# Gate/up blocks with four quads each, two pairs of the up half split by ScalarE and an adding DMA

## The chip, the cores and the metric

One core of a Trainium2 chip runs the whole layer. The metric is the device time of one execution in microseconds (us); lower is better. Durations in the text come from one profiled execution of the kernel before.

## What is computed

The input x has 256 tokens of 2048 channels. Three stages follow each other, each with a norm ahead of it and behind it and a residual sum: a feed-forward stage, a mixer (a recurrent branch and a pooling branch) and a second feed-forward stage. The change touches the gate and up products of the two feed-forward stages:

```
f = (silu(u @ w_gate) * (u @ w_up)) @ w_down     # u: 256 x 2048, normed
                                                 # w_gate, w_up: 2048 x 5632, w_down: 5632 x 2048
h = h + 0.5 * rmsnorm(f) * g
```

## The kernel before

**Products in three parts.** All weights are float32. TensorE multiplies them in its float32r form, which keeps fewer bits, so each operand is split into a high part H (the value rounded to float32r) and a low part L = value - H. A product of two tiles is three matmuls into one PSUM bank (`mm3`, L313 to L315): H by H, L by H, H by L. The weight is the moving operand: 128 rows by 512 columns, against 128 tokens.

**How a weight tile comes in.** `fetch` (L356) handles a *pair*: two neighbouring groups of 128 weight rows by 512 columns. SP loads the 512 KB (`get_w`, L275), ScalarE writes H as a rounding copy (`cast`, L367), VectorE subtracts for L (`low`, L370). The load goes into one of four w32 buffers or a spare *unit* (a 128 x 1024 tile from a pool of 33); H and L go into a ring of five buffers, or, with `hold`, into two units of their own.

**Gate/up blocks.** The 5632 columns are 11 blocks of 512. Block 0 is a plain product. Blocks 1 to 10 go through `seven` (L482 on), which computes one block of gate (f) and of up (l) together for both halves of the 256 tokens, four output tiles of 128 x 512. The string in `GATE_UP` gives the order within a block: `f` is a pair of gate (12 matmuls), `l` a pair of up, `q` a *quad*. A quad takes two groups of 128 rows of both gate and up and computes what a pair of each would, but with seven products in place of eight: 21 matmuls against 24. For that it needs sums and differences of the weights. SP loads four pieces of 256 KB (L545), VectorE makes t13 (L550, 1024 per partition), and the two halves of t24 (L555 and L559, 512 each), ScalarE casts four operands (L567) and VectorE subtracts for four low parts (L572, three of 1024 and one of 512). With n quads a block has 8 - n pairs of f and of l. Blocks 2, 4, 6, 8 and 10 have three quads, blocks 3, 5, 7 and 9 four.

**The rest of a block.** `merge` copies the first finished product (L614, ScalarE, once per block) and adds others to it (L619, six additions per block, VectorE); `total` (L666) closes the up half. Then come silu (L1020), the product of both halves (L1027), a transposition in 32 x 32 squares (L848, VectorE), sixteen moves of 32 KB between partitions by GpSimd's DMAs (`move`, L865), and the split of the result into H and L (L878 ScalarE, L882 VectorE), which stays in units as the operand of the down product.

**What sets the order.** A planner (`Plan`, L87 on) lists every instruction of these stages as a node with an engine, an assumed duration, its inputs, the buffers it takes and frees, and a due time counted back from TensorE's order, which is fixed. `solve` (L134) places the nodes one by one: on each engine the one that can start first, by due time where several can. The instructions of PE, ScalarE, VectorE and SP are then emitted in that order (`run`, L261). GpSimd is not among the engines of that hand-made schedule; its order is left to the framework. For a DMA the planner assumes a start `LEAVE` after the issue, a rate of `RATE` MB per us on one shared line, and `LAND` until the data can be used.

Of the kernel before, what the change touches and what calls it, by code (L numbers as in the profile page):

```python
# [10 lines left out]
F32 = mybir.dt.float32  # L11
# [45 lines left out]

ROWS = [("ln_mix_pre", 16), ("ln_ffn2_pre", 16), ("mu", 26), ("w0", 8), ("a0", 8),
        ("k_k", 8), ("k_a", 8)]
# [27 lines left out]
class Plan:  # L87
# [46 lines left out]
    def solve(s):  # L134
        succ = {n: [] for n in s.nodes}
        for n in s.nodes:
            for d in n.deps:
                succ[d].append(n)
        for n in reversed(s.nodes):
            for m in succ[n]:  # L140
                if n.eng == "PE":
                    break
                v = m.due - n.dur - (n.lat + (EARLY if m.eng == "PE" else 0.0)
                                     if m.eng != n.eng else 0.0)
# [70 lines left out]
class Block:  # L215
# [45 lines left out]
    def run(s):  # L261

        E = mybir.EngineType
        with s.tc.manual_schedule(engines={E.PE, E.Activation, E.DVE, E.SP}):
            for n in s.plan.solve():
                n.fn()
            s.stats()
        s.plan, s.ready = Plan(), {}
# [84 lines left out]
            for h in range(2):  # L353
                evac(h, pss[h])

    def fetch(s, w, k, c0, keep, hold=False):  # L356

        p, x = s.plan, {}
        src = Tok("w32", "unit")
        dst = [Tok("unit"), Tok("unit")] if hold else [Tok("ring")]  # L360

        def load():
            x["w"] = s.get_w(w, k, 2, c0, 512, own=src.of == "unit")

        def cast():
            x["v"], x["H"], x["L"] = s.halves_of(x["w"], hold)
            s.nc.scalar.copy(x["H"], x["v"])  # L367

        def low():
            s.nc.vector.tensor_tensor(out=x["L"], in0=x["v"], in1=x["H"].bitcast(F32),  # L370
                                      op=ALU.subtract)
# [110 lines left out]
    def seven(s, wf, cf, wl, cl, at, dep, KT, need, sm, order, ev_f, ev_l, used, trail=0):  # L482
# [32 lines left out]
        def keep(tiles):  # L515
            ws.update((k, (wH, wL)) for k, wH, wL in tiles)

        def pair(k, w, c0, b):
            low, dst = s.fetch(w, k, c0, keep)

            def do():
                for i in range(2):
# [6 lines left out]
        def quad(q):  # L529
# [40 lines left out]
            def low(n_, m):  # L570
# [1 line left out]
                V.tensor_tensor(out=L, in0=src, in1=H.bitcast(F32), op=ALU.subtract)  # L572
                x[n_] = [(H[:, i], L[:, i]) for i in range(m)]
            ld = [p.op("SP", 0.4, lambda m=m: get(m), take=([ka], [kb], (), ())[m], size=0.26,
                       chain="SP") for m in range(4)]

            def half(n_, m, deps, rel):
                ring = Tok("ring")
# [56 lines left out]
        for c in order:  # L635
            if c == "q":
                last["q"] = quad(nq)
                nq += 1
                if nq == n:
                    merge(last["q"])  # L640
                    if "f" in m:
                        close_f()
                continue
            w_ = (wf, cf) if c == "f" else (wl, cl)
            last[c] = pair(next(ks[c]), *w_, c)
# [208 lines left out]
    def carry_steps(s, T1, T, x32=None):  # L854
# [1 line left out]
        nc = s.nc  # L856
        x, own = [x32], []

        def move():
            if x32 is None:  # L860
                x[0] = s.unit((P, 4, 2, 4, 32), F32, "x32")
            src = s.blocks(T1[0])
            for i in range(4):
                for q in range(4):
                    nc.gpsimd.dma_start(out=x[0][q * 32:q * 32 + 32, i],  # L865
                                        in_=src[i * 32:i * 32 + 32, q])
# [26 lines left out]
    def carry(s, T1, T, turned, k1):  # L893
# [1061 lines left out]
```

## Time and profile before

| | us |
|---|---|
| median of 3 runs | 2025.65 (2025.48 to 2026.15) |
| the profiled execution | 2025.32 |
| its span, first to last instruction | 2023.6 |

The profile gives for each engine its busy time and, for groups of equal instructions, the count and mean duration; the chain that ended last; the windows, which are busy times of each engine in a stretch of the span; and the timeline, which has single instructions with their start and length. Lines such as L370 are lines of the kernel before. Matmuls overlap on TensorE and VectorE's instructions overlap a little, so the distance of two starts is the price of an instruction in a full engine, and the duration is more than that.

### The profile page before, as it was taken

What the parts mean: (1) busy time and instruction counts of PE and PEld (TensorE: products, weight loads), DVE (VectorE), ACT (ScalarE), POOL (GpSimd) and SP (SyncE); (2) the same over time, 40 slices, a digit from 0 to 9 for tenths busy, and PEclk for the clock granted to TensorE, in tenths of its full rate; (3) what the DMA queues carried; (4) which work ended last, traced back from release to release, by engine and by line L of the source; (5) the groups of instructions that cost most, each with busy time, mean ns of one, the idle gap of its engine ahead of it and who ended that gap; (6) DMA issues with size and microseconds to landing.
All of it is one profiled execution on the core that took longest, in us unless ns stands there. A gap on an engine that the chain in (4) does not pass through costs nothing.

```text
span 2023.6 us, 28609 instructions
## 1 busy us (share of the span) xinstructions
PE 2008.3 (99%) x9987; PEld 1660.2 (82%) x9987; DVE 1774.4 (88%) x2344; ACT 1180.8 (58%) x1575; POOL 325.2 (16%) x673
## 2 busy tenths in 40 slices
PE   9999999999999999999999999999999999999997
PEld 7888888888888888888788788888888888888886
DVE  6999999999989857799689577779999999999896
ACT  7565665655655566685576434565566556566553
POOL 0111211121000123403220111011112111210000
PEclk9999999999999999999999999999999999999999
DMA  7757475577567677757456558756574755775674
GB/s 267 254 179 265 148 253 188 186 221 245 185 204 268 225 204 214 204 175 216 147 169 187 160 169 278 245 196 232 187 266 151 246 190 183 223 243 189 203 261 145
DMA packets 227098, 423.55 MB, mean 209 GB/s; under 512 B 24320, under 2 KB 27786, under 8 KB 226954
## 3 DMA queue, kind: packets, MB, share of 16 engines
q1 hardware_dynamic: 204393, 384.70, 58.5%
q0 software_dynamic: 22272, 36.51, 5.5%
q8 instruction: 78, 1.28, 0.3%
q10 hardware_dynamic: 288, 0.52, 0.1%
q14 instruction: 67, 0.54, 0.1%
HBM read 396.69 MB, written 8.39 MB: 200 GB/s over the span
## 4 chain that ended last, share of the span: by engine, by line
PE 98%; issue 1%; DVE 1%; ACT 0%; DMA 0%; DVEq 0%; POOLq 0%; POOL 0%; SPq 0%; ACTq 0%
PE mm L313 27%; PE mm L315 27%; PE mm L314 27%; PE ms L313 4%; PE ms L315 4%; PE ms L314 4%; PE tr L822 0%; PE pA L1673 0%; PE mc L790 0%; PE pU L1769 0%; DMA w<-in_ffn_gate_dram 0%; PE pSa L1781 0%; PE pY L1804 0%; DVE xL L840 0%; PE pT L1840 0%
## 5 line engine op out<-in xcount | busy, mean ns | idle before, releaser
L313 PE MATMUL mm<-wH,xH 128*128 128x512 f32 (+1 forms) x2184 | 851.5, 391 | 0.4 <-ACT xH L831 0.4
L315 PE MATMUL mm<-wH,xL 128*128 128x512 f32 (+1 forms) x2184 | 847.8, 388 | 1.6 <-DVE xL L840 1.6
L314 PE MATMUL mm<-wL,xH 128*128 128x512 f32 (+1 forms) x2184 | 847.5, 388 | 0.0
L367 ACT CAST wH<-w 128x1024 fp32r<-128x1024 f32 x333 | 346.8, 1053 | 239.7 <-PE mm L315 209.2
L315 PEld LDWEIGHTS mm<-wH,xL 128*128 128x128 f32 x2184 | 409.9, 188 | 87.5 <-DVE xL L840 3.2
L313 PEld LDWEIGHTS mm<-wH,xH 128*128 128x128 f32 x2184 | 410.0, 188 | 85.5 <-ACT xH L831 1.0
L314 PEld LDWEIGHTS mm<-wL,xH 128*128 128x128 f32 x2184 | 410.1, 188 | 82.3
L370 DVE TENSOR_TENSOR wL<-w,wH 128x1024 fp32r<-128x1024 f32 x333 | 396.9, 1217 | 39.5 <-ACT wH L367 36.5
L567 ACT CAST wH<-t 128x1024 fp32r<-128x1024 f32 x188 | 198.2, 1054 | 222.8 <-PE mm L315 156.5
L290 DVE TENSOR_TENSOR wL<-w,wH 128x1024 fp32r<-128x1024 f32 (+2 forms) x202 | 239.0, 1192 | 96.5 <-ACT wH L289 93.3
L289 ACT CAST wH<-w 128x1024 fp32r<-128x1024 f32 (+2 forms) x202 | 207.7, 1034 | 164.5 <-PE mm L315 142.9
L865 POOL DMA_DIRECT2D x<-T x352 | 172.5, 498 | 748.4 <-DVE T L848 394.9
L572 DVE TENSOR_TENSOR wL<-t,wH 128x1024 fp32r<-128x1024 f32 x188 | 225.5, 1217 | 14.1 <-ACT wH L567 13.9
L567 ACT CAST wH<-w 128x1024 fp32r<-128x1024 f32 (+1 forms) x188 | 153.6, 835 | 48.4 <-PE mm L315 40.3
L572 DVE TENSOR_TENSOR wL<-w,wH 128x1024 fp32r<-128x1024 f32 (+1 forms) x188 | 175.6, 950 | 2.4 <-ACT wH L567 2.4
L550 DVE TENSOR_TENSOR t<-w,w 128x1024 f32<-128x1024 f32 x94 | 114.4, 1217 | 0.7 <-DMA w<-in_ffn_down_dram 0.7
L313 PE MATMUL ms<-wH,sH 128*128 128x512 f32 x252 | 98.0, 389 | 0.0
L314 PE MATMUL ms<-wL,sH 128*128 128x512 f32 x252 | 98.0, 389 | 0.0
L315 PE MATMUL ms<-wH,sL 128*128 128x512 f32 x252 | 98.0, 389 | 0.0
L559 DVE TENSOR_TENSOR t<-w,t 128x512 f32<-128x512 f32 x94 | 64.8, 689 | 2.1
L555 DVE TENSOR_TENSOR t<-w,t 128x512 f32<-128x512 f32 x94 | 64.3, 684 | 0.8
L619 DVE TENSOR_TENSOR u<-ms,u 128x512 f32<-128x512 f32 x92 | 61.3, 685 | 1.6
(311 smaller groups left out, 2017.6 us busy)
## 6 DMA issues: line engine op xcount, KB each, us to landing
w<-in_w_in_dram SPq DMA_DIRECT2D x128, 512.0 KB
w<-in_ffn_down_dram SPq DMA_DIRECT2D x116, 512.0 KB
w<-in_ffn_up_dram SPq DMA_DIRECT2D x114, 512.0 KB
w<-in_ffn_gate_dram SPq DMA_DIRECT2D x112, 512.0 KB
w<-in_ffn_gate_dram SPq DMA_DIRECT2D x128, 256.0 KB
w<-in_ffn_up_dram SPq DMA_DIRECT2D x124, 256.0 KB
w<-in_ffn_down_dram SPq DMA_DIRECT2D x120, 256.0 KB
w<-in_w_out_dram SPq DMA_DIRECT2D x28, 512.0 KB
```

The source lines that it names most:

```text
L289: s.nc.scalar.copy(vH, v)
L290: s.nc.vector.tensor_tensor(out=vL, in0=v, in1=vH.bitcast(F32), op=ALU.subtract)
L313: nc.tensor.matmul(ps, aH, bH, start=start, stop=False)
L314: nc.tensor.matmul(ps, aH, bL, start=False, stop=False)
L315: nc.tensor.matmul(ps, aL, bH, start=False, stop=stop)
L367: s.nc.scalar.copy(x["H"], x["v"])
L370: s.nc.vector.tensor_tensor(out=x["L"], in0=x["v"], in1=x["H"].bitcast(F32), op=ALU.subtract)
L550: V.tensor_tensor(out=v["t13"], in0=v["a"], in1=v["b"][:, :1].to_broadcast([P, 2, 512]), op=ALU.subtract)
L559: V.tensor_tensor(out=v["t24"][:, 1], in0=v["b"][:, 1], in1=v["t24"][:, 0], op=ALU.subtract)
L567: nc.scalar.copy(H, src)
L572: V.tensor_tensor(out=L, in0=src, in1=H.bitcast(F32), op=ALU.subtract)
L865: nc.gpsimd.dma_start(out=x[0][q * 32:q * 32 + 32, i], in_=src[i * 32:i * 32 + 32, q])
```

## The change

Blocks 2 to 9 all have the order `ffqfqfqlqLLl`: four quads, four pairs of gate, and four pairs of up, of which two, written `L`, get their low part in another way. ScalarE writes H as before and then -1 times the weight, rounded, into the tile of L (that is -H); a DMA that GpSimd issues then adds the same weights, read once more from DRAM, to that tile, so it holds value - H. VectorE has no part in it. These two pairs have H and L in units of their own (`hold`), not in the ring, and their casts are not in the chain that keeps the other casts in order.

Beside it: GpSimd joins the engines whose order the planner writes out; the sixteen moves of a block become four steps of four; a load may be placed no earlier than `FETCH` = 22 us ahead of its due time; due times ahead of a DMA count its assumed transfer; a DMA that is not SP's does not wait in SP's line in the plan (but takes it up); and `RATE` is 0.28 in place of 0.25.

```diff
-GATE_UP = ["", "ffffffffllllllll"] + ["fffqffqllqlll", "ffqfqfqlqlll"] * 4 + ["fffqffqllqlll"]
+GATE_UP = ["", "ffffffffllllllll"] + ["ffqfqfqlqLLl"] * 8 + ["fffqffqllqlll"]
-SOON, LATEST, BEFORE = 22.0, 12.0, 12.0
+SOON, FETCH, LATEST, BEFORE = 22.0, 22.0, 12.0, 12.0
-RATE, LEAVE, LAND = 0.25, 1.05, 2.0
+RATE, LEAVE, LAND = 0.28, 1.05, 2.0
...
         for n in reversed(s.nodes):
+            lat = max(n.lat, n.size and LEAVE + n.size / RATE + LAND)
...
-                line = max(n.free + LEAVE, line) + n.size / RATE
-                n.end = max(n.end, line + LAND)
+                start = max(n.free + LEAVE, line)
+                line = start + n.size / RATE
+                n.end = max(n.end, (line if n.eng == "SP" else n.free + LEAVE + n.size / RATE)
+                            + LAND)
...
-        with s.tc.manual_schedule(engines={E.PE, E.Activation, E.DVE, E.SP}):
+        with s.tc.manual_schedule(engines={E.PE, E.Activation, E.DVE, E.SP, E.Pool}):
...
+        def minus():
+            nc.scalar.activation(out=x["L"], in_=x["v"], func=AF.Copy, scale=-1.0)
+
         def low():
-            s.nc.vector.tensor_tensor(out=x["L"], in0=x["v"], in1=x["H"].bitcast(F32),
-                                      op=ALU.subtract)
+            if by_dma:
+                nc.gpsimd.dma_start(out=x["L"], in_=w[k * P:(k + 2) * P, c0:c0 + 512]
+                                    .rearrange("(k p) c -> p k c", p=P), accum_op=ALU.add)
+            else:
+                nc.vector.tensor_tensor(out=x["L"], in0=x["v"], in1=x["H"].bitcast(F32),
+                                        op=ALU.subtract)
...
-        n = p.op("SP", 0.4, load, take=[src], size=0.52, chain="SP")
-        n = p.op("ACT", cost("ACT", 1024), cast, [n], take=dst, chain="cast")
+        n = p.op("SP", 0.4, load, take=[src], size=0.52, chain="SP", ahead=FETCH)
+        n = p.op("ACT", cost("ACT", 1024), cast, [n], take=dst,
+                 chain=None if by_dma else "cast")
+        if by_dma:
+            n = p.op("ACT", cost("ACT", 1024), minus, [n], rel=[src])
+            return p.op("POOL", 1.0, low, [n], size=0.94, lat=0.0), dst
...
-        n = p.op("POOL", 10.0, move, turned, [kx], [k1], chain="carry", spare=2, lat=8.0)
+        n = None
+        for i in range(4):
+            n = p.op("POOL", 2.5, lambda i=i: move(i), [*turned, n], [kx] if i == 0 else (),
+                     [k1] if i == 3 else (), chain="carry", spare=2, lat=8.0)
```

More of the change, by code (lines that the diff above doesn't have):

```diff
@@ L142, in solve @@
                     break
-                v = m.due - n.dur - (n.lat + (EARLY if m.eng == "PE" else 0.0)
+                v = m.due - n.dur - (lat + (EARLY if m.eng == "PE" else 0.0)
                                      if m.eng != n.eng else 0.0)
@@ L354, in gemm_tok, with fetch @@
                 evac(h, pss[h])
-    def fetch(s, w, k, c0, keep, hold=False):
-        p, x = s.plan, {}
+    def fetch(s, w, k, c0, keep, hold=False, by_dma=False):
+        nc, p, x = s.nc, s.plan, {}
         src = Tok("w32", "unit")
@@ L366, in cast @@
             x["v"], x["H"], x["L"] = s.halves_of(x["w"], hold)
-            s.nc.scalar.copy(x["H"], x["v"])
+            nc.scalar.copy(x["H"], x["v"])
+        def minus():
+            nc.scalar.activation(out=x["L"], in_=x["v"], func=AF.Copy, scale=-1.0)
         def low():
-            s.nc.vector.tensor_tensor(out=x["L"], in0=x["v"], in1=x["H"].bitcast(F32),
-                                      op=ALU.subtract)
-            keep([(k + i, x["H"][:, i], x["L"][:, i]) for i in range(2)])
-        n = p.op("SP", 0.4, load, take=[src], size=0.52, chain="SP")
-        n = p.op("ACT", cost("ACT", 1024), cast, [n], take=dst, chain="cast")
+            if by_dma:
[4 more added lines that the diff above has]
+                                        op=ALU.subtract)
+            keep([(k + i, x["H"][:, i], x["L"][:, i]) for i in range(2)])
+        n = p.op("SP", 0.4, load, take=[src], size=0.52, chain="SP", ahead=FETCH)
[4 more added lines that the diff above has]
+            return p.op("POOL", 1.0, low, [n], size=0.94, lat=0.0), dst
         return p.op("DVE", cost("DVE", 1024), low, [n], rel=[src]), dst
@@ L516, in keep, with pair @@
             ws.update((k, (wH, wL)) for k, wH, wL in tiles)
-        def pair(k, w, c0, b):
-            low, dst = s.fetch(w, k, c0, keep)
+        def pair(k, w, c0, b, by_dma):
+            low, dst = s.fetch(w, k, c0, keep, by_dma, by_dma)
             def do():
@@ L574, in quad @@
             ld = [p.op("SP", 0.4, lambda m=m: get(m), take=([ka], [kb], (), ())[m], size=0.26,
-                       chain="SP") for m in range(4)]
+                       chain="SP", ahead=FETCH) for m in range(4)]
             def half(n_, m, deps, rel):
@@ L643, in seven @@
                 continue
+            by_dma, c = c in "FL", c.lower()
             w_ = (wf, cf) if c == "f" else (wl, cl)
-            last[c] = pair(next(ks[c]), *w_, c)
+            last[c] = pair(next(ks[c]), *w_, c, by_dma)
             left[c] = left.get(c, 0) + 1
@@ L857, in carry_steps, with move @@
         x, own = [x32], []
-        def move():
-            if x32 is None:
+        def move(*part):
+            if x[0] is None:
                 x[0] = s.unit((P, 4, 2, 4, 32), F32, "x32")
             src = s.blocks(T1[0])
-            for i in range(4):
+            for i in part or range(4):
                 for q in range(4):
```

## Prediction

> **What bounds the kernel now.** I read the page's busy times and its chain first, then the windows of single gate/up blocks, then the timelines of TensorE and VectorE inside one block.
>
> ```profile
> span 2023.6 us, 28609 instructions
> PE 2008.3 (99%) x9987; PEld 1660.2 (82%) x9987; DVE 1774.4 (88%) x2344; ACT 1180.8 (58%) x1575; POOL 325.2 (16%) x673
> PE 98%; issue 1%; DVE 1%; ACT 0%; DMA 0%; DVEq 0%; POOLq 0%; POOL 0%; SPq 0%; ACTq 0%
> ```
>
> The chain that ends last is TensorE for 98% of the span, so a matmul taken away is worth its spacing on TensorE, as long as nothing else becomes late. The mean of 390 ns that the groups give for a matmul is no spacing, since matmuls overlap. Two rows of TensorE's timeline, 54 matmuls apart, give it: (72.34 - 60.10) / 54 = 0.2267 us.
>
> ```profile
> 60.10 0.39 PE L313 MATMUL mm<-wH,xH 128*128 128x512 f32 x1
> 72.34 0.39 PE L313 MATMUL mm<-wH,xH 128*128 128x512 f32 x1
> ```
>
> The blocks that the change touches can be cut apart at L614, which copies the first finished product once per block.
>
> ```profile
> 131.98 0.58 ACT L614 COPY u<-ms 128x512 f32<-128x512 f32 x1
> 172.78 0.57 ACT L614 COPY u<-ms 128x512 f32<-128x512 f32 x1
> 214.26 0.58 ACT L614 COPY u<-ms 128x512 f32<-128x512 f32 x1
> ```
>
> A quad is 7 products of 3 matmuls, a pair 12 matmuls. A block with four quads and eight pairs has 180 matmuls, 40.80 us by the spacing; one with three and ten has 183, 41.48 us. The copies stand 40.80 and 41.48 us apart: TensorE does not wait at all in these blocks. Now the same stretches by engine (the columns are the length, then busy time and instructions of PE, PEld, DVE, ACT, POOL, then clock, DMA share, GB/s):
>
> ```profile
> 131.98:172.78 40.80, 40.80 (x182) 33.78 (x181) 40.63 (x48) 25.72 (x30) 7.81 (x16) 1.00 0.64 220
> 172.78:214.26 41.48, 41.48 (x185) 34.35 (x184) 41.20 (x48) 23.09 (x27) 7.82 (x16) 1.00 0.61 200
> ```
>
> VectorE is busy for 40.63 of 40.80 and 41.20 of 41.48 us. The 88% of the page hides that: **here two engines are full at once**, TensorE and VectorE. ScalarE has 15 us free per block, GpSimd 33, the DMA engines a third of their time.
>
> **The change part by part.** *TensorE.* The eight blocks 2 to 9 go from three or four quads to four. Four of them gain a quad, in two feed-forward passes: 8 quads more, each saving 3 matmuls (21 in place of 24), 24 matmuls in all; the order of the changed program has 24 matmuls fewer. 24 x 0.2267 = **5.44 us less**.
>
> *VectorE.* Its price per instruction is the spacing of starts, not the duration:
>
> ```profile
> 343.20 1.28 DVE L619 TENSOR_TENSOR u<-mm,u 128x512 f32<-128x512 f32 x2
> 344.40 2.35 DVE L370 TENSOR_TENSOR wL<-w,wH 128x1024 fp32r<-128x1024 f32 x2
> 346.67 1.22 DVE L550 TENSOR_TENSOR t<-w,w 128x1024 f32<-128x1024 f32 x1
> ...
> 348.94 0.68 DVE L555 TENSOR_TENSOR t<-w,t 128x512 f32<-128x512 f32 x1
> 349.65 0.69 DVE L559 TENSOR_TENSOR t<-w,t 128x512 f32<-128x512 f32 x1
> 350.26 1.28 DVE L666 TENSOR_TENSOR u<-mm,u 128x512 f32<-128x512 f32 x2
> ```
>
> Two of 512 take 344.40 - 343.20 = 1.20, so 0.60 each; two of 1024 take 2.27, so 1.135. L559 needs L555's result and starts 0.71 behind it: 0.11 lost per quad. A quad has four of 1024 and three of 512: 4.54 + 1.80 + 0.11 = 6.45. A pair has one of 1024: 1.135. The rest of a block is fourteen of 512: six L619, two each of L666, L1027, L848 and L882, as the groups' counts over 23 blocks with quads, 18 feed-forward blocks and 22 transposed ones show:
>
> ```profile
> L619 DVE TENSOR_TENSOR u<-ms,u 128x512 f32<-128x512 f32 x92 | 61.3, 685 | 1.6
> L666 DVE TENSOR_TENSOR u<-mm,u 128x512 f32<-128x512 f32 x46 | 29.8, 681 | 13.9 <-PE mm L315 13.9
> L619 DVE TENSOR_TENSOR u<-mm,u 128x512 f32<-128x512 f32 x46 | 29.4, 679 | 0.0
> L882 DVE TENSOR_TENSOR xL<-x,xH 128x512 fp32r<-128x512 f32 x44 | 29.4, 678 | 0.0
> L848 DVE STREAM_TRANSPOSE T<-u 128x512 f32<-128x512 f32 x36 | 25.2, 704 | 0.6
> L1027 DVE TENSOR_TENSOR u<-u,u 128x512 f32<-128x512 f32 x36 | 24.2, 671 | 0.0
> ```
>
> 14 x 0.60 = 8.4, with some 0.05 of gaps. Before, a block of three quads and ten pairs: 19.35 + 11.35 + 8.45 = 39.15; of four and eight: 25.8 + 9.08 + 8.45 = 43.33. Two neighbours need 82.48 against TensorE's 82.28: VectorE loses 0.2 us per two blocks. After, a block has four quads and eight pairs, of which two give up their subtraction: 25.8 + 6.81 + 8.45 = 41.06 against 40.80: it loses 0.26 per block. Over eight blocks that is 0.8 us lost before and 2.1 after, so VectorE comes out 1.3 us later at the end of them. It works ahead of TensorE, and this lead is what pays. How much is left of it:
>
> ```profile
> 367.32 2.35 DVE L370 TENSOR_TENSOR wL<-w,wH 128x1024 fp32r<-128x1024 f32 x2
> ...
> 369.05 0.39 PE L314 MATMUL mm<-wL,xH 128*128 128x512 f32 x1
> ```
>
> The first of the two L370 (by the order, the low part that this L314 reads) ends at 368.54, 0.51 us ahead of its use; it is the smallest margin in blocks 2 to 9. So the extra 1.3 us outrun it by 0.8 at such dips; with the new order of pairs and quads I take **1.0 us of waiting per pass, 2.0 in all** (from 0, if the two pairs without VectorE work come where it is short, to 2 x 2.1 = 4.2, if no lead is left). The wait is TensorE's, at a low part; everything behind it moves by as much.
>
> *ScalarE.* It gains 32 negatives and 8 x 4 casts for quads less 16 for pairs.
>
> ```profile
> L367 ACT CAST wH<-w 128x1024 fp32r<-128x1024 f32 x333 | 346.8, 1053 | 239.7 <-PE mm L315 209.2
> ```
>
> By this row at most 32 x 1.05 + 8 x 4 x 1.05 - 16 x 1.05 = 50 us, 3 per block, in 15 us of free time: nothing, as long as it casts for VectorE in time; it mostly waits for ring tiles that TensorE frees.
>
> *SP and GpSimd.* SP issues 16 loads more (four of 256 KB per quad for two of 512 KB, the same bytes). A load now waits until 22 us ahead of its due time; the 32 adding DMAs read 16.8 MB more, 4% of the 396.69 MB that are read now. GpSimd's own queue is now written out by the planner; the sixteen moves of a block, which used to be one step, are four, and adding DMAs may stand between them.
>
> ```profile
> L865 POOL DMA_DIRECT2D x<-T x123: 496/496/498, 119.5 to 429.8; - x123
> DMA to landing us min/median/max: 1.6/4.1/7.6
> L1105 POOL DMA_DIRECT2D gb<-in_ln_ffn_post_dram x4: 543/558/568, 633.5 to 1957.8; - x4
> DMA to landing us min/median/max: 5.2/6.9/8.0
> DMA to landing us min/median/max: 3.9/6.1/8.4
> q1 hardware_dynamic: 204393, 384.70, 58.5%
> HBM read 396.69 MB, written 8.39 MB: 200 GB/s over the span
> ```
>
> Two issues of some 0.56 us per block beside 7.8 us of moves: nothing by themselves. The moves' issue time of 496 to 498 ns holds while VectorE is full, so the two engines do not slow each other here. What an **adding transfer** of 512 KB takes, no row shows. The nearest are plain ones of 512 KB from GpSimd: L1105's six land in 5.2 to 8.0 us, L1895's twelve (the last landing line) in 3.9 to 8.4. A packet takes 0.585 x 16 x 2023.6 / 204393 = 0.093 us, and 256 packets on 16 engines make 1.5 us; if adding passes the data twice, 6.9 + 1.5 = 8.4 us. I take that; the ends are 3.9 (as the quickest plain one) and 13.8 (all of 6.9 doubled).
>
> How long the kernel can wait for it I count in the changed order: the cast ahead of each negative waits for a ring tile that a matmul frees, and from that matmul to the first product with the low part stand 68 and 62 matmuls in blocks 2, 5, 7 and 8, 80 and 80 in 3, 101 and 92 in 4, 74 and 68 in 6, 56 and 62 in 9. Less the two or three ScalarE instructions of up to 1.05 us between, the lead is 12.3 to 13.3 and 10.9 to 12.0 us in most blocks, and least in block 9: 56 x 0.2267 - 3.2 = 9.5. At 8.4 us no adding DMA is late: **0**. TensorE alone waits for it, and it is the only thing then late.
>
> The Trainium skill, "DMA: Bandwidth & Descriptors", section "Rules for kernel authors", speaks against the change here: an accumulating DMA reads its destination and writes it later, so it is not a plain write. No run here shows its time; by that rule alone the transfer is somewhere between my 8.4 and the doubled 13.8, and it is why the third case below has the chance that it has.
>
> **Sum.** The profiled execution took 2025.32 us, its span 2023.6; 2025.32 - 5.44 + 2.0 + 0 = 2021.9. The median of the runs is 0.33 above it: **2022.3 us**, 3.4 less than 2025.65.
>
> **The rivals.** *VectorE keeps up* (0 in place of 2.0): 2020.2. For it speaks that a stretch of 36 matmuls, 8.2 us (the two pairs in a row and the pair behind them), asks VectorE for one subtraction only; against it the 0.51 us margin and the 0.26 per block.
>
> *The adding DMA is late* (the case on the other side). Place: the first product with a low part of the two pairs, in blocks 9, 8, 7, 5 and 2 in this order. Price: what the landing exceeds the lead by, the second pair's less what the first has already waited. At 13 us it is 1.0 in blocks 2, 5 and 7, 2.1 in 8, 3.5 in 9, 8.6 per pass, 17.2 in two; TensorE's wait lets VectorE catch up, so its 2.0 fall away: 2025.65 - 5.44 + 17.2 = 2037.4. It eats the gain from about 11.6 us on (0.7 in block 8 and 2.1 in 9, 5.6 in two passes). For it: a landing of 8.4 was seen for a plain transfer, and 4% more bytes go through the same engines. Against it: 30% of DMA time free.
>
> *The change does not do what it says*: weight loads, now asked for at most 22 us ahead and sharing the engines with the adding DMAs, come late, and VectorE's saved 2.3 us per block are lost to casts that wait. If each second block lost 1 us: 8 in two passes, 2028.
>
> **How the numbers follow.** My forecast 0.40 (its own range 2020.9 to 2024.5), VectorE keeps up 0.22, an adding DMA late by a little (10 to 12 us, 2021 to 2029) 0.10, late by more (2030 to 2046) 0.22, late loads 0.06. The range 2020.0 to 2034.0 leaves out 0.05 below and some 0.14 above. About 0.2%, 4.05 us, is what a measurement of this kernel can tell from no change: faster holds the second case and 0.04 of the first, 0.26; same the rest of the first, the little lateness and 0.02 of the late loads, 0.48; slower what is left, 0.26.
>
> **What would show it.** L614 copies 40.80 us apart in all of blocks 2 to 9 prove that nothing waits; longer ones place the wait. TensorE's wait at L317 (the product with the low part) names VectorE if the forecast holds, the adding DMA if the third case does. The adding DMAs' landing tells 8.4 from 13.8. VectorE should stay above 99% in these windows, ScalarE rise by 3 us. Wrong I am if the landing passes 11.6 us, or if copies show 40.80 throughout.

## The result: slower by 0.6%

| | before | after |
|---|---|---|
| median of 5 runs each, us | 2025.65 (2025.38 to 2026.15) | 2038.31 (2032.88 to 2039.67) |
| ratio, 95% interval | | 1.0058 (1.0044 to 1.0071) |
| the profiled execution, us | 2025.32 | 2036.59 |
| its span, us | 2023.6 | 2034.9 |

The time lies above the range; it is where the third case, the late adding DMA, was priced (2037.4). First the page of after, the lines that answer to those shown of before:

```profile
span 2034.9 us, 28738 instructions
...
PE 2007.4 (99%) x9963; PEld 1655.4 (81%) x9963; DVE 1772.2 (87%) x2352; ACT 1216.0 (60%) x1623; POOL 366.6 (18%) x705
...
PE 64%; DVE 13%; DMA 9%; issue 6%; POOL 1%; ACT 1%; DVEq 0%; SPq 0%; POOLq 0%; ACTq 0%
```

The busy times hardly move: there are 24 matmuls fewer (9963 for 9987), and TensorE still counts as 99% busy. What moved is the chain: TensorE held 98% of it, now 64%, and VectorE and the DMAs hold 22%. The chain follows each wait back to its releaser, so one wait of 2 us can turn a long stretch of it over to others; it says that the path has changed, not how much was lost. For that, the windows, again from one L628 to the next (the line that was L614), with the same columns as in the prediction:

```profile
131.16:173.79 42.63, 41.10 (x182) 33.72 (x181) 41.90 (x50) 27.23 (x33) 7.28 (x12) 1.00 0.75 221
173.79:214.58 40.79, 40.79 (x182) 33.78 (x181) 40.01 (x47) 27.09 (x32) 13.48 (x25) 1.00 0.79 233
```

The second of them is what the prediction drew: 40.8 us, TensorE without a gap. The first is 1.8 us longer. TensorE's waits name what ended them (us in all, times, longest):

```profile
PE mm L317 <- DMA kL<-in_ffn_up_dram: 7.8, 5, 2.1
...
PE mm L317 <- DVE wL L380: 0.7, 1, 0.7
...
PE ms L317 <- DVE wL L586: 0.6, 2, 0.4
```

By the distance of starts above 0.2267 us they are somewhat longer: 9.2 us for the adding DMAs, with the 0.11 that each costs the matmul behind it (the second pairs of blocks 2, 5 and 9 in the first feed-forward pass: 1.69, 0.86, 1.99; of blocks 2 and 9 in the second: 1.81, 2.28; one more of 0.06), and 1.2 for VectorE in these blocks. One of them in the timeline, block 9 of the second pass. The first row is a cast that waited for a matmul to free its tile; the negative is the seventh of seven ScalarE instructions that follow each other from there without a gap. Then come the adding DMA and the product that needs it:

```profile
1724.23 1.06 ACT L581 CAST wH<-t 128x1024 fp32r<-128x1024 f32 x1 [1.41 <-PE mm L318]
...
1729.93 1.06 ACT L373 ACTIVATE kL<-w 128x1024 fp32r<-128x1024 f32 x1
...
1731.30 1.20 POOL L377 DMA_DIRECT2D kL<-in_ffn_up_dram  x1 [1.61 <-ACT kL L373]
...
1739.47 0.39 PE L316 MATMUL mm<-kH,xH 128*128 128x512 f32 x1
1741.98 0.50 PE L317 MATMUL mm<-kL,xH 128*128 128x512 f32 x1 [2.12 <-DMA kL<-in_ffn_up_dram]
...
1743.67 0.63 PE L317 MATMUL mm<-kL,xH 128*128 128x512 f32 x1
1744.09 0.63 PE L318 MATMUL mm<-kH,xL 128*128 128x512 f32 x1
```

TensorE could have used the low part at 1739.70, 8.4 us behind the issue; it got it at 1741.98. The last two rows stand 0.42 us apart in place of 0.23: the clock had dropped. Three windows, the last number but two being the clock and the last but one the share of DMA time:

```profile
195.40:205.85 10.45, 10.45 (x48) 8.66 (x47) 10.45 (x13) 9.73 (x12) 3.44 (x4) 1.00 0.67 101
1731.30:1741.90 10.60, 8.37 (x36) 6.29 (x34) 10.50 (x14) 4.58 (x6) 4.24 (x8) 1.00 1.05 274
1743.20:1746.60 3.40, 3.40 (x9) 2.63 (x8) 1.26 (x2) 2.58 (x4) 2.26 (x5) 0.50 0.91 293
```

The first is the flight of block 4's two adding DMAs, which landed in 6.5 and 6.0 us; the second that of the late one just shown, 10.6. Where it was late the DMA engines were full by this measure. Over all 32, each from its issue to its landing, the eleven that took more than 9 us flew at shares of 1.04 to 1.09, and the seven that took 6.5 us or less at 0.59 to 0.82. The third is the slow clock, 3.4 us at half, which costs 8 matmuls some 0.2 us each, 1.6 us. Landing and issue of the adding DMAs over the whole run (ns of the issue; then us to landing):

```profile
L377 POOL DMA_DIRECT2D kL<-in_ffn_up_dram x32: 1178/1249/1340, 121.8 to 1731.3; - x32
...
DMA to landing us min/median/max: 5.9/8.0/10.6
```

Last, the closing drain of GpSimd (the minimum, median and maximum of its drains, ns), of before and of after:

```profile
L1950 POOLq DRAIN  x3: 46/93/8191, 2014.6 to 2023.4; - x3
```

```profile
L1968 POOLq DRAIN  x3: 46/98/10803, 2023.3 to 2034.6; - x3
```

It starts with GpSimd's last instruction and all engines wait for its end; it is 2.6 us longer. The account of the 11.3 us of span: -5.44 (matmuls) + 9.2 (adding DMAs) + 1.6 (slow clock) + 1.2 (VectorE in the blocks) + 1.6 (waits at low parts in the last down product, 2001.9 to 2006.5) + 2.6 (drain) = 10.8. The other 0.5 is spread over steps of a few hundredths; the start has no part in it, since after is 0.1 us ahead of before there.

### The profile page after: what moved, and what is told of

Same layout as the page of the kernel before. It is cut to its first block, busy times and chain, and to the rows that moved or that the text cites. A ratio compares the mean times of both kernels' runs of the same rounds, so it can differ in the third digit from the quotient of the medians.

```text
span 2034.9 us, 28738 instructions
## 1 busy us (share of the span) xinstructions
PE 2007.4 (99%) x9963; PEld 1655.4 (81%) x9963; DVE 1772.2 (87%) x2352; ACT 1216.0 (60%) x1623; POOL 366.6 (18%) x705
## 4 chain that ended last, share of the span: by engine, by line
PE 64%; DVE 13%; DMA 9%; issue 6%; POOL 1%; ACT 1%; DVEq 0%; SPq 0%; POOLq 0%; ACTq 0%
PE mm L316 18%; PE mm L317 18%; PE mm L318 18%; DVE wL L586 4%; DMA kL<-in_ffn_up_dram 4%; DVE wL L380 2%; PE ms L317 2%; PE ms L316 2%; PE ms L318 2%; DMA x<-T 2%; DVE t L564 2%; DMA w<-in_ffn_gate_dram 1%; DMA w<-in_ffn_down_dram 1%; DVE t L569 1%; POOL x L880 1%
## 5 line engine op out<-in xcount | busy, mean ns | idle before, releaser
L316 PE MATMUL mm<-wH,xH 128*128 128x512 f32 (+1 forms) x2008 | 783.3, 391 | 0.4 <-ACT xH L846 0.4
L318 PE MATMUL mm<-wH,xL 128*128 128x512 f32 (+1 forms) x2008 | 779.3, 388 | 1.6 <-DVE xL L855 1.6
L317 PE MATMUL mm<-wL,xH 128*128 128x512 f32 (+1 forms) x2008 | 779.5, 388 | 0.8 <-DVE wL L380 0.7
L316 PEld LDWEIGHTS mm<-wH,xH 128*128 128x128 f32 x2008 | 376.9, 188 | 79.0 <-ACT xH L846 1.0
L317 PEld LDWEIGHTS mm<-wL,xH 128*128 128x128 f32 x2008 | 377.3, 188 | 77.2 <-DVE wL L380 1.7
L370 ACT CAST wH<-w 128x1024 fp32r<-128x1024 f32 x285 | 297.4, 1053 | 224.8 <-PE mm L318 181.9
L380 DVE TENSOR_TENSOR wL<-w,wH 128x1024 fp32r<-128x1024 f32 x285 | 341.9, 1219 | 49.9 <-ACT wH L370 47.0
L581 ACT CAST wH<-t 128x1024 fp32r<-128x1024 f32 x204 | 213.6, 1053 | 192.6 <-PE mm L318 138.0
L586 DVE TENSOR_TENSOR wL<-t,wH 128x1024 fp32r<-128x1024 f32 x204 | 244.2, 1219 | 16.0 <-ACT wH L581 15.6
L581 ACT CAST wH<-w 128x1024 fp32r<-128x1024 f32 x204 | 165.6, 834 | 55.1 <-PE mm L318 35.0
L586 DVE TENSOR_TENSOR wL<-w,wH 128x1024 fp32r<-128x1024 f32 x204 | 190.0, 950 | 0.0
L377 POOL DMA_DIRECT2D kL<-in_ffn_up_dram x32 | 39.7, 1240 | 368.6 <-ACT kL L373 201.3
L317 PE MATMUL mm<-kL,xH 128*128 128x512 f32 x164 | 65.1, 397 | 7.8 <-DMA kL<-in_ffn_up_dram 7.8
L573 DVE TENSOR_TENSOR t<-w,t 128x512 f32<-128x512 f32 x102 | 70.3, 690 | 2.4
```

The lines of the kernel that those rows point to most:

```text
L316: nc.tensor.matmul(ps, aH, bH, start=start, stop=False)
L317: nc.tensor.matmul(ps, aH, bL, start=False, stop=False)
L318: nc.tensor.matmul(ps, aL, bH, start=False, stop=stop)
L573: V.tensor_tensor(out=v["t24"][:, 1], in0=v["b"][:, 1], in1=v["t24"][:, 0], op=ALU.subtract)
L581: nc.scalar.copy(H, src)
```

## The experiments

The theory, A: the adding DMAs come later than TensorE needs them, a slow clock follows, and the drain grows with GpSimd's DMAs. The rival, B: the side changes (planner, GpSimd's order, late loads) or VectorE cost it. All times are in us, medians of 4 to 11 runs, against the kernel before on the same chip; edits are shown against the changed kernel.

| kernel | median | ratio (95%) |
|---|---|---|
| side changes alone | 2026.14 | 1.0003 (0.9994 to 1.0012) |
| no adding DMA | 2022.84 | 0.9985 (0.9976 to 0.9994) |
| plain DMA | 2026.45 | 1.0003 (0.9994 to 1.0012) |
| planner's size 1.6 | 2068.88 | 1.0216 (1.0202 to 1.0230) |
| adding DMA ahead of moves | 2037.23 | 1.0056 (1.0042 to 1.0069) |
| none in block 9 | 2030.62 | 1.0027 (1.0017 to 1.0037) |
| early drain | 2034.19 | 1.0045 (1.0031 to 1.0058) |
| these three together | 2024.85 | 0.9997 (0.9988 to 1.0005) |
| GpSimd subtracts | 2089.01 | 1.0316 (1.0301 to 1.0330) |
| VectorE subtracts all | 2051.36 | 1.0128 (1.0114 to 1.0142) |
| halves of 256 KB | 2030.05 | 1.0020 (1.0011 to 1.0029) |
| before, with a drain | 2025.66 | 0.9998 (0.9989 to 1.0007) |
| the three, and halves | 2028.55 | 1.0014 (1.0005 to 1.0023) |
| blocks 2 to 7, halves | 2024.62 | 0.9997 (0.9988 to 1.0006) |
| side changes, early drain | 2024.81 | 0.9998 (0.9989 to 1.0006) |
| planner told 9.0 us | 2056.35 | 1.0152 (1.0138 to 1.0166) |
| blocks 2 to 7, whole | 2027.70 | 1.0007 (0.9998 to 1.0016) |
| blocks 3 to 7, whole | 2023.94 | 0.9991 (0.9982 to 1.0000) |

### Which part costs

**Side changes alone:**

```diff
-["ffqfqfqlqLLl"] * 8
+["fffqffqllqlll", "ffqfqfqlqlll"] * 4
```

> This kernel is the changed one with the order of pairs and quads of before: no adding DMA and no quad more, only the planner's side changes (GpSimd in the written order, moves in four steps, loads at most 22 us ahead, the faster assumed rate). Theory A (the adding DMAs come later than TensorE needs them, 9 us of waits with the slow clock behind one of them, and GpSimd's closing drain is 2.6 us longer because it has had more DMAs): nothing of that is in here, so 2025 to 2027 us, the closing drain some 8.2 us, and no matmul waits in blocks 2 to 9. Theory B (the side changes cost it: late loads, or VectorE served in a worse order): most of the 13 us lost against the forecast is in here, 2031 us or more.

The time is 2026.14, no matmul of the gate/up blocks waits for more than 0.1 us, and the drain takes 8.19. The half of rival B that blames the side changes falls.

**No adding DMA:**

```diff
-                nc.gpsimd.dma_start(out=x["L"], in_=w[k * P:(k + 2) * P, c0:c0 + 512]
-                                    .rearrange("(k p) c -> p k c", p=P), accum_op=ALU.add)
+                pass
```

> The changed kernel with the 32 adding DMAs left out: the low part of those pairs stays minus the high part, and everything else, each engine's order too, is as in the changed kernel. Theory A: what is left is 24 matmuls fewer and VectorE's waits, 1.2 us by the trace of after: 2025.65 - 5.44 + 1.2 = 2021.4 us (2020.5 to 2023), the closing drain back at 8.2 us, TensorE's clock without a drop, waits in blocks 2 to 9 of at most 1.5 us. Theory B: the waits move to VectorE or to the loads, 2029 us or more.

The time is 2022.84, the drain takes 8.19, and the clock does not drop. TensorE's waits:

```profile
PE mm L317 <- DVE wL L379: 1.2, 3, 0.7
```

By starts it is 0.6 us in the blocks of each pass, and 1.5 in the last down product. So VectorE costs 1.2 in the blocks, where the prediction took 2.0. The transfers cost 15.5 us (2038.31 - 2022.84): the 12.7 between before and after, and the gain of 2.8 that stands here.

**Plain DMA:**

```diff
-                                    .rearrange("(k p) c -> p k c", p=P), accum_op=ALU.add)
+                                    .rearrange("(k p) c -> p k c", p=P))
```

> The changed kernel with the 32 DMAs writing the weights plainly instead of adding them (the low part of those pairs is then the whole weight). Same order, same number and bytes of DMAs. Theory A with the adding as the cause of the late landing: landing some 6 to 7 us instead of 8.0 and at most 8.4 instead of 10.6, waits for these DMAs from 7.8 to under 1.5 us, no clock drop; the closing drain stays at 10.8 if the number of DMAs sets it: 2021.4 + 2.6 + 0.5 = 2024.5 (2023.5 to 2027). If the queues and the bytes set the landing and not the adding: as the changed kernel, 2034 to 2039. Theory B: 2034 to 2039 with waits elsewhere.

```profile
DMA to landing us min/median/max: 3.8/5.0/9.4
```

```profile
PE mm L317 <- DMA kL<-in_ffn_up_dram: 1.0, 2, 0.6
```

The time is 2026.45, the drain 10.80. The same bytes at the same places land in 5.0 us in place of 8.0, are issued in 0.73 us in place of 1.25, and TensorE's waits for them fall from 7.8 to 1.0. So the adding itself is 3 us of the landing, and lateness is what costs. The drain is as long with plain DMAs as with adding ones. The Trainium skill, "DMA: Bandwidth & Descriptors", section "Rules for kernel authors", the rule weighed in the prediction (an accumulating DMA reads its destination and writes it later), gives no time for it; that it is no plain write agrees with these 3 us.

### What makes it late

**Adding DMA ahead of moves** (behind the planner's order):

```diff
+        for n in [n for n in order if n.eng == "POOL" and n.size]:
+            i = order.index(n)
+            j = i - 1
+            while order[j].eng != "POOL":
+                j -= 1
+            m = order[j]
+            if not m.size and m.start > n.start - 6.0 and not set(succ[m]) & set(order[j:i]):
+                order[j:i + 1] = order[j + 1:i + 1] + [m]
```

> The changed kernel; only GpSimd's order differs: where four moves stand directly ahead of an adding DMA in its queue, the adding DMA goes first. In the profile of after this queue held the adding DMAs of block 2 by 2.7 and 3.5 us behind their negatives and the second one of block 5 by 1.9. Theory A1 (the lead is lost in GpSimd's queue there): those waits go, 1.8 + 1.0 us in the first pass and 1.9 + 0.1 in the second; block 9, whose DMAs were issued 0.3 us behind the negatives, keeps its 2.1 and 2.4 with the slow clock of 1.6 behind the second: 2038.3 - 4.8 = 2033.5 us (2032 to 2035). Theory A2 (the landing is set by what the DMA engines have to do, not by the issue): landings stay where they were, 2037 to 2039.

2037.23: by the time A1 fails and A2 comes close. But this execution is 2.3 us later than that of after already at its start, ahead of the changed blocks, so the waits have to decide. Block 2 of the second pass, where after had issued at 1443.46 and used at 1453.32:

```profile
1441.06 1.62 POOL L390 DMA_DIRECT2D kL<-in_ffn_up_dram  x1
...
1453.29 0.50 PE L330 MATMUL mm<-kL,xH 128*128 128x512 f32 x1 [1.03 <-DMA kL<-in_ffn_up_dram]
```

Issued 2.4 us earlier, it took 12.2 us to land in place of 9.8, and the wait by starts fell only from 1.81 to 1.19. Of the waits that A1 expected to go, only block 5's went, and block 8 got one of 1.0. In this stretch, where the DMA engines are full (share 1.09), an earlier issue bought little.

**None in block 9:**

```diff
-["ffqfqfqlqLLl"] * 8
+["ffqfqfqlqLLl"] * 7 + ["ffqfqfqlqlll"]
```

> The changed kernel, but block 9 has its four quads and no adding DMA, as before the change, so 28 adding DMAs are left. Theory A: the two waits of block 9 go (2.1 and 2.4) and the slow clock of 1.6 us behind the second; the closing drain falls by 2.6 x 4 / 32 = 0.3; VectorE has 2.3 us more to do in that block and TensorE waits for it by up to 1 us per pass: 2038.3 - 6.4 + 1 = 2033 (2031.5 to 2035). If the wait there is only a symptom of a backlog that moves on: 2036 to 2039.

2030.62, a little better than expected: block 9's waits and the wait of the last down product are gone, and TensorE does not wait for VectorE there. The slow clock came in block 2 of the second pass instead, behind waits of 1.0 and 2.1 us that end 5 us apart. The drain, 10.48, is as expected for 28.

**The planner asked for more time**, twice: `size=1.6`, and `lat=9.0` with the size as it was.

```diff
-            return p.op("POOL", 1.0, low, [n], size=0.94, lat=0.0), dst
+            return p.op("POOL", 1.0, low, [n], size=1.6, lat=0.0), dst
```

> The changed kernel with one assumption of the planner changed: an adding DMA counts as 1.6 MB in place of 0.94 on its line, so the load, cast and negative ahead of it are due 0.66 / 0.28 = 2.4 us earlier. Theory A: the waits for adding DMAs fall from 7.8 us to under 2, the slow clock goes with them, the drain stays at 10.8: 2021.4 + 2.6 + 1 = 2025 (2024 to 2029). If ring tiles and ScalarE's order fix the issue whatever the plan wants: no change, 2034 to 2039. Theory B: no change or slower.

> The changed kernel where the planner is told that an adding DMA takes 9.0 us from GpSimd's issue (it counts 6.4 from its size and rate), while what it takes up of the assumed line stays at 0.94 MB. The earlier try took up more of that line: 2 x 5.7 us of adding DMAs and 8.39 MB / 0.28 = 30.0 us of loads are 41.4 us per block against TensorE's 40.8, so the plan's own loads fell behind. Theory A with that reading: with the line free, the negatives come some 2.6 us earlier and the waits go, 2026 to 2030 us. Rival (tiles, of which a pair in waiting holds two, run short towards block 9, so the plan can't start earlier and only moves other work): 2040 us or more.

2068.88 and 2056.35, both far worse than any theory of the first said. In the first TensorE waits 14.2 us for adding DMAs and 16.0 for casts (L581). In the second, block 8 of the first pass:

```profile
375.86 1.26 POOL L377 DMA_DIRECT2D kL<-in_ffn_up_dram  x1 [1.14 <-ACT kL L373]
```

```profile
379.38 0.39 PE L316 MATMUL mm<-kH,xH 128*128 128x512 f32 x1
385.19 0.79 PE L317 MATMUL mm<-kL,xH 128*128 128x512 f32 x1 [5.42 <-DMA kL<-in_ffn_up_dram]
```

Told to allow 9.0 us, the planner left 3.7 (379.61 - 375.86). So its assumption of 6.4 us was not the cause by itself: asking for more does not give it. The rival of the second run, that the planner has no tiles for a longer wait, would fit this. It would also fit that after's leads shrink from 19.6 us in block 4 to 8.6 in block 9 (the first pair of the first pass, from issue to use), while the products of finished blocks fill the units. Which resource ran out was not measured.

**Halves of 256 KB:**

```diff
-                nc.gpsimd.dma_start(out=x["L"], in_=w[k * P:(k + 2) * P, c0:c0 + 512]
-                                    .rearrange("(k p) c -> p k c", p=P), accum_op=ALU.add)
+                for i in range(2):
+                    nc.gpsimd.dma_start(out=x["L"][:, i], in_=w[(k + i) * P:(k + i + 1) * P,
+                                                                c0:c0 + 512], accum_op=ALU.add)
```

> The changed kernel with each adding DMA cut into two of 256 KB, so 64 of them with the same packets and bytes in all. On the closing drain: 10.8 us if packets or bytes set it, some 13.4 if each DMA costs 0.08 us. On the landing: the half that TensorE needs first can be used when it has landed, perhaps 1 us earlier than the whole, but GpSimd issues twice: 2036 to 2040 us if the drain is by DMAs, 2030 to 2036 if it is by packets and the halves help.

```profile
PE mm L317 <- DMA kL<-in_ffn_up_dram: 1.8, 3, 1.1
...
PE mm L317 <- DVE wL L587: 1.3, 2, 0.6
PE ms L317 <- DVE wL L587: 1.2, 4, 0.4
PE mm L316 <- DVE u L634: 1.1, 2, 0.6
```

2030.05, 8.3 us less than the changed kernel; 4.0 of them lie behind the last matmul, where the closing drain no longer sets the end. The halves land in 6.6 us (median) and most of the lateness goes; but now TensorE waits for VectorE, 3.6 us in this view. This fits what the prediction said of the third case: a wait for a DMA gives VectorE time to catch up, and when it goes, VectorE is late next. The drain did neither of the two things expected:

```profile
L1969 POOLq DRAIN  x3: 46/93/3529, 2020.4 to 2027.7; - x3
```

### The closing drain

An instruction more, behind GpSimd's last DMAs (in `load_to`), in the changed kernel, in the kernel before, and in the side changes alone:

```diff
+                if last:
+                    nc.gpsimd.drain()
```

> The changed kernel with one more instruction: a drain of GpSimd behind its last DMAs, some 35 us ahead of the end, where it has nothing to do. Theory: the closing drain of 10.80 us is work that has piled up with GpSimd's DMAs (8.19 us at 576 of them, 10.80 at 608) and runs from GpSimd's last instruction on. Then the early drain takes it over with some 10 us, the closing one is under 2 us, and the end is set by the output's landing, 4.1 us earlier: 2034.2 us. Rival: the closing drain is a fixed cost of ending a program with so many DMAs: as the changed kernel, 2038 us, both drains long.

> The kernel before with one more instruction, the early drain of GpSimd behind its last DMAs. By the run of the changed kernel with it, the closing drain falls from 8.19 to some 0.7 us and the end is set by the output's landing, 1.7 us earlier: 2023.9 us. If in the kernel before something else ends as late: 2025.6.

> The order of pairs and quads of before with the planner's side changes (GpSimd's order is written out, so a drain stays where it is put) and the early drain: no adding DMA. The control for the versions with the early drain: 2026.1 - 1.7 = 2024.4 us, the closing drain under 1 us. What those versions gain beyond that comes from the 24 matmuls.

```profile
L1916 POOLq DRAIN  x1: 15121/15121/15121, 1984.5 to 1984.5; - x1
```

```profile
L1970 POOLq DRAIN  x3: 34/93/658, 2024.3 to 2031.6; - x3
```

In the changed kernel the early drain took 15.1 us where GpSimd had nothing to do, the closing one 0.66, and the time fell by 4.1 to 2034.19, as expected. In the kernel before, GpSimd's order is the framework's, which put the drain at 3.2 us, where it takes 0.44; so that run tests nothing (2025.66, where 2023.9 was expected). The side changes with it gave 2024.81, 1.3 less than without. So it is shown that the drain is work left over from GpSimd's DMAs that can be done earlier. What sets its length is open, since 64 halves left 3.53.

### Other hands for the low part

**VectorE subtracts all:**

```diff
-["ffqfqfqlqLLl"] * 8
+["ffqfqfqlqlll"] * 8
```

> The changed kernel with all low parts from VectorE: four quads in all eight blocks, no adding DMA. Theory (VectorE is full beside TensorE: 43.33 us of work per such block against 40.80): 2.5 us lost per block but for the lead, 16 blocks, so 20 to 38 us of waits: 2040 to 2058 us. If VectorE has more room than the prediction said: 2020 to 2030.

2051.36, as expected: four quads in all blocks do overload VectorE, and the 32 pairs taken off it are needed. Of the loss, 3.7 us lie in the mixer and have another cause (see the versions).

**GpSimd subtracts:**

```diff
-                nc.gpsimd.dma_start(out=x["L"], in_=w[k * P:(k + 2) * P, c0:c0 + 512]
-                                    .rearrange("(k p) c -> p k c", p=P), accum_op=ALU.add)
+                nc.gpsimd.tensor_tensor(out=x["L"], in0=x["v"], in1=x["H"].bitcast(F32),
+                                        op=ALU.subtract)
...
-            n = p.op("ACT", cost("ACT", 1024), minus, [n], rel=[src])
-            return p.op("POOL", 1.0, low, [n], size=0.94, lat=0.0), dst
+            return p.op("POOL", 2.5, low, [n], rel=[src], lat=0.2), dst
```

> The two pairs of each block get their low part from GpSimd instead: a subtraction of 128 x 1024 in place of the negative and the adding DMA. No transfer, and nothing of the computation is left out. Theory A (what the change loses is the transfer's lateness and the drain it adds; the division of VectorE's work is sound): waits for adding DMAs and the longer drain are gone, 2025.65 - 5.44 + 1.2 = 2021.4 us (2020 to 2024), if GpSimd's subtraction does not slow VectorE. If it does (each of some 2.5 us holding VectorE up in full: 5 us per block against the 2.3 saved, 16 blocks): 2065 us or more, VectorE's mean subtraction above 1.22 us; then the adding DMA is what it takes to leave VectorE alone.

```profile
150.72 2.82 POOL L377 TENSOR_TENSOR kL<-w,kH 128x1024 fp32r<-128x1024 f32 x1 [23.10 <-ACT kH L370]
```

```profile
149.44 0.69 DVE L568 TENSOR_TENSOR t<-w,t 128x512 f32<-128x512 f32 x1
...
151.19 2.90 DVE L572 TENSOR_TENSOR t<-w,t 128x512 f32<-128x512 f32 x1
```

2089.01. VectorE's instruction of 512, started 0.5 us behind GpSimd's, takes 2.90 us in place of 0.69 and ends behind it: these two do not work side by side. The Trainium skill, "SBUF — State Buffer", section "Who interferes with whom", says that a VectorE instruction with two SBUF inputs contends with a GpSimd instruction that reads SBUF; the trace agrees. GpSimd's DMA issues, by contrast, did not slow VectorE (L380 takes 1219 ns at the median and 1227 at most in after).

### Versions

The three edits together (adding DMA ahead of moves, none in block 9, early drain), then with halves, then with fewer blocks: 2 to 7 with halves, 2 to 7 whole, 3 to 7 whole with the planner told 9.5 us.

```diff
-["ffqfqfqlqLLl"] * 7 + ["ffqfqfqlqlll"]
+["ffqfqfqlqLLl"] * 6 + ["ffqfqfqlqlll"] * 2
...
+["ffqfqfqlqlll"] + ["ffqfqfqlqLLl"] * 5 + ["fffqffqllqlll", "ffqfqfqlqlll"]
```

> The three edits together: adding DMAs ahead of moves, block 9 without them, the early drain. Theory A with the drain as piled-up work: no wait for an adding DMA above 0.5 us, no slow clock, the closing drain hidden: 2038.3 - 4.8 - 6.4 + 1 - 4.1 = 2024.0 (2020.5 to 2025.5); a bound from below is the 2022.8 of the kernel without adding DMAs less 1.7 for its drain, 2021.1. Theory B (something else of the change costs what is lost): 2030 or more.

> The three edits together (adding DMAs ahead of moves, block 9 without them, the early drain) and each adding DMA cut into two of 256 KB. Without the cut, these edits left 1.4 us of waits for adding DMAs, all for the second one of block 2. If the cut's halves help as in the kernel that has the cut alone: under 0.5 us of such waits, 2023 us (2021 to 2024.5), below the kernel before. If the cut helped there by something else (its short closing drain): as without it, 2025.

> As the one with the cut and the three edits, but block 8 too has no adding DMA (four quads, all subtractions on VectorE), so 24 pairs are left with VectorE spared. The second adding DMA of block 8 landed 10.2 to 11.0 us behind its issue in nearly every kernel. If lateness is what matters: no wait for adding DMAs, 2022.5 us (2021 to 2024). If VectorE, with two such blocks in a row (2 x 2.5 us short, less the lead), is what matters: 2025 to 2028.

> Adding DMAs whole again (512 KB), in blocks 2 to 7 only (24 of them), ahead of moves, with the early drain; blocks 8 and 9 have four quads and all subtractions on VectorE. The same with halves of 256 KB had 1.3 us of waits in the two passes, but one stretch of the mixer, which the change does not touch, was 3.7 us longer there. If that stretch was an accident of that program: -5.44 + 1.7 (waits) - 1.7 (drain) from 2025.65, 2020.2 us (2020 to 2022.5), below both kernels. If it comes again, or the second adding DMA of block 2 is late as in the kernel with seven blocks (0.7 and 1.0): 2023.5 to 2025.

> Adding DMAs in blocks 3 to 7 only (20), none in blocks 2, 8 and 9, of which block 8 has three quads (6 matmuls more in two passes than with four); ahead of moves, early drain, and the planner told 9.5 us for an adding DMA. By their leads (above 10 us in blocks 3 to 7) no adding DMA is late: waits for them 0; VectorE's waits 1 to 2.5 us; 2025.65 - 4.08 + 2 - 1.7 = 2021.9 us (2020.5 to 2024). If late DMAs appear in other blocks once the planner asks for more time, as with 9.0 us in all eight blocks: 2030 or more.

```profile
PE mm L330 <- DMA kL<-in_ffn_up_dram: 1.4, 2, 0.8
```

The three edits gave 2024.85 with 1.4 us of waits for adding DMAs left (the row above), as expected: 13.5 of the loss are undone by what theory A names, the drain's 4.1 among them.

The others did not add up. Halves on top gave 2028.55: the waits for DMAs are 0.4, but VectorE's came instead in the first pass, and the early drain had already taken what the halves gain at the end.

Blocks 2 to 7 gave 2024.62 with halves, between the two cases expected (2021 to 2024, 2025 to 2028), and 2027.70 whole, above both (2020 to 2022.5, 2023.5 to 2025). In both, a stretch of the mixer (878 to 921) that the change does not touch is 3.7 us longer, as with VectorE subtracting all and the planner told 9.0. TensorE waits there for results of VectorE (blocks 2 to 7 with halves; in the kernel before it does not wait in this stretch at all):

```profile
PE pA L1705 <- DVE R L1681: 1.3, 2, 1.1
PE pB L1724 <- DVE R L1716: 1.1, 2, 0.8
```

In this stretch the instructions of VectorE and of ScalarE stand in one order in these four kernels and in another in all the rest, before among them; TensorE's order is the same in all. In the four, a subtraction of a weight's low part has come ahead of the results that TensorE waits for. So the 3.7 us go with another order in the mixer. Why the planner chose it is open, and no run has these blocks with the usual order. As an estimate, less the 3.7, the two kernels would be at 2020.9 and 2024.0, the first below the kernel before.

Blocks 3 to 7 gave 2023.94, with no wait for an adding DMA at all. By its trace the idea leaves 1.7 us there: 18 matmuls fewer, 4.1 us, less 2.4 of waits for VectorE in the two passes. The medians can't tell this from nothing: none of these kernels is faster than the kernel before by more than can be told, and the side changes with the drain alone give 2024.81.

## Why the prediction was wrong

- **24 matmuls, 5.44 us less:** right (the counts, and 40.79 us for an undisturbed block).
- **VectorE, 2.0 us:** right in kind, and somewhat too large: 1.2 in the blocks, with the DMAs and without. What was not in the sum is 1.5 more of waits at low parts in the last down product, there with the DMAs and without, gone in the run that has none in block 9 (0.7 with the three edits together).
- **ScalarE, SP, GpSimd, nothing:** right as far as none of them is full. An adding DMA's issue is 1.25 us, not 0.56; no wait of TensorE is put down to that. But the queues of ScalarE and GpSimd shorten the lead (next point). "Against it: 30% of DMA time free" was wrong as a reason: that is a mean, and where the late ones flew the share was 1.04 to 1.09.
- **The failed step: "At 8.4 us no adding DMA is late: 0".** The landing was well taken as a median, 8.0, but the two things made of it failed. One landing stood for all, and the late ones took 9.5 to 10.6 us, in the full stretches. And the lead was counted from the matmul that frees the ring tile, less at most three ScalarE instructions. That gave 10.9 us or more for block 9's second pair, where it was 8.4: the tile was free at 1725.64 by this count, but ScalarE, busy without a gap since 1724.23, came to the cast ahead of the negative at 1728.05. For block 2's second pair it was 7.8, with GpSimd's moves 3.5 us ahead of the issue, which the part on GpSimd had named and priced at nothing. By the price of the third case, landing less lead, 10.6 - 8.4 gives the wait of 2.2 that is there. With a lead of 10.9 the same landing would have been in time, though the run with the adding DMAs ahead of the moves shows that an earlier issue can also land more slowly.
- **The point of the third case, 11.6 us,** was therefore too far off: the waits ate the gain with landings of 9.5 to 10.6. That its time, 2037.4, came out near the measured one is luck, since the terms are others: 9.2 us of waits, not 17.2, and 1.6 of slow clock, 1.6 in the last down product and 2.6 of drain, which were in no case.
- **The third rival, late loads,** did not happen: the side changes alone give the time of before.
- **The sign, copies 40.80 us apart,** was unfit for the later blocks: in the kernel before, where no matmul of blocks 2 to 9 waits, the last three distances of the first pass are 41.99, 39.78 and 42.88.

Without the DMAs the kernel takes 2022.84, against the forecast's 2022.3 (its terms add up to 2022.2). That is near in part by luck, since 0.8 too much for VectorE in the blocks made up for half of the 1.5 that was not in the sum. What was wrong by far is the zero for the transfers.

## What to carry to other kernels

A transfer that replaces an engine's work has to be judged by its slowest landing in the stretch where it flies: read the DMA share of that window, not of the span, and take the lead from the real issue to the use, with everything that stands ahead of it in the issuing queue. A planner's assumed latency is no lead; here, asking for more made other things late. Where two engines are full, removing a wait on a third can just show the next. And a planner can change its order in a stage that the edit does not touch, so compare that stage too before a time is put down to the edit.

## What the runs showed of the hardware

- **Adding costs time:** 512 KB from DRAM added to a tile land in 8.0 us at the median (5.9 to 10.6), written plainly at the same places in 5.0 (3.8 to 9.4).
- **A short wait can halve the clock.** TensorE ran at 0.50 for 3.4 us behind a wait of 2.28 us (2.12 idle in the row above). Of the twenty waits of 2.27 us or more (by starts, from the first gate/up blocks on) in all these runs, nineteen were followed by the slow clock; one of 2.63, with the planner told 9.0 us, was not. Of the shorter ones (up to 2.17), only some that came within 5 us of another wait were. The Trainium skill, "TensorE: Matmul & The Clock Gate", section "Part 1: The HAM clock gate", has the half clock come after an idle window of about 3.4 us; here less was enough.
- **GpSimd's closing drain** is 8.19 us with 576 DMAs, 10.48 with 604, 10.80 with 608 (adding or plain), but 3.53 with 640 of which 64 are halves. A drain issued ahead of the end, where GpSimd is idle, leaves 0.66 of it.
- **The start** of the profiled executions differs: by its 60th instruction TensorE is 3.5 us later than in before in the three edits together and 3.0 later with blocks 3 to 7, though nothing there was changed; why is open. The profiled execution with blocks 3 to 7 was the slowest of its eleven (2025.90; the fastest took 2022.90), so part of the spread may lie there.
